# RWKV pairs of a hybrid decoder block: one written list orders the steps of three pairs and the weight stream on all engines

## The chip, the cores and the metric

One Trainium2 chip, one core of it. The metric is the device time of one launch of the kernel in microseconds. Times in tables and traces are microseconds unless marked ns. TensorE multiplies, ScalarE (ACT) and VectorE (DVE) work element by element, GpSimd (POOL) and SyncE (SP) mostly issue transfers here. Each engine takes its instructions in the order in which the program lists them for it, and semaphores make one engine wait for another.

## What is computed

One residual block for a sequence of 512 rows and 2048 channels in fp32. Cut to what matters:

```python
h = rms_norm(x, norm1_g)
z = h @ w_in                                   # 2048 x (RWKV 3*1024+96+96+256, attention 1536, gates 4096)
zs = token_shift(z[..., :RW], rw_mu)           # z + (z_prev - z) * mu
r, k, v, wd, ad, gd = split(zs)
decay = exp(-exp(-softplus(-(w0 + tanh(wd) @ w2)) - 0.5))
a = sigmoid(a0 + ad @ a2);  g = sigmoid(gd) @ g2
kk = normalised(k * k_k);   k = k * (1 + (a - 1) * k_a)
# per head of 64, over the 512 steps:
state = state * w_t + (state @ -kk_t) * (kk_t a_t) + v_t k_t;   y_t = state @ r_t
o_rw = (group_norm(y) + sum(r * k * r_k) * v) * g
o_att = sliding_window_attention(z)
p = sigmoid(zg1) * (o_rw @ w_branch[:1024]) + sigmoid(zg2) * (o_att @ w_branch[1024:])
x = x + p @ w_out
x = x + conv_ffn(rms_norm(x, norm2_g))
```

The change touches the recurrence with its normalisation (o_rw), and the products `h @ w_in` that run beside it.

## The kernel before, in words

The launch goes through stages: the norm and the first products with the attention (up to about 262 us), the RWKV stage (331 to 1168 us), the branch product with w_branch (from 1168 us, "stage B" here), then w_out and the convolutional feed-forward. The change lies in the RWKV stage and in the way into stage B.

**fp32 products.** Every fp32 operand is split into two parts that TensorE multiplies at full rate: hi, a rounded copy that ACT makes, and lo, the remainder that DVE makes by a subtraction. A product is then three matmuls, hi by hi, hi by lo, lo by hi (lines 255, 256, 257). The weights of w_in come as tiles `raw` of 128 x 512 (256 KB) by SP; `load_w` (230) splits one into `whi` (ACT, 238) and `wlo` (DVE, 239), and `project` (244) runs the twelve matmuls (128x512, here "products") that one raw tile feeds. One group of 128 columns of z is four raw tiles, 48 products, into a bank `acc`.

**Pairs.** The sixteen heads are worked in eight pairs of 128 channels, the sequence in NCH = 8 chunks of C = 64 steps. For each pair p there are three functions, and the loop at their end calls late(0), early(1), final(0), three gates, late(1), and so on:

- `early(p)` (from 635): the columns k, r and v of the pair (144 products), the token shift (`shifted`: ACT to `zpad`, DVE to `kz`, `rz`, `vz`), the norm of the key (`head_stats`, a small rsqrt on DVE `rq`, the transposed rows `rsT` that go through DRAM, `rsb`), the low-rank parts of decay and rate, their scans and exponentials (`Ei`, `Et`), and the bonus `bon`.
- `late(p)` (from 690): `BKK` and `BAR`, the two operands of the chunk-wise products; `gram` (719), the 64x64 products within a chunk, masked by DVE to `OW` and `AM` (722); the inverse of a triangular matrix by doubling. Its first level comes from `OW` directly; the transposes of `OW` (729) become `at` (733), split to `AI`, masked to `BT` (741). Then come five levels of two passes. A pass is `mm3` (16 small fp16 matmuls, lines 773 and 774, into the two halves of a PSUM bank) and a DVE `reduce_sum` over the halves (776, 'half'). The first pass (on AI) is masked (790), cast (791) and its remainder taken (792); the second (on BT) scales one half of the result into `BX` on ACT (794) and the other on DVE (795), refreshes `XIW` (797 on ACT, 798 on DVE), and the transposes `id,XIW` (802) are copied back to BT (DVE 806, ACT 808). Beside that DVE scales the keys, `BKK<-BKK,ee` (742, 128x1024), TensorE transposes them (758), ACT copies them to `KD` and `KO` (762, 763); `vz` is transposed and centred (`vm`, `VV`, 746 to 752). Last comes the serial chain over the eight chunks (814 to 828).
- `final(p)` (from 833): outputs of the chunks, their statistics, the scaling `yd` (851), its transposes (855), group norm, the gate's low-rank product `lora6` (618 to 620) and the store `o_rw_d` by POOL (861).

Between them `emit_gate` (357) makes one group of gate columns: 48 products, a tanh on ACT (`gt`, 363), a store. Three gates go with each pair, so a pair holds 6 x 48 = 288 products. The rest comes at the end of the stage: four gates, then the outputs `rin` and the attention's outputs `ain` are loaded by POOL (881, 883) and split (`rhi`, `rlo`, `ahi`, `alo`, 885 to 893) with a gate after every second split.

**Who sets the order.** A list scheduler orders the instructions of each engine by its own estimate of times. Only what is wrapped in `pin` keeps its order in the source among pinned instructions of its engine (the gram, the small matmuls of `heads_mm`, the products of a chain, the splits of stage B). The bank pools: `blk_ps` with 3 banks for everything named `bulk`, `chn_ps` with 2 for the chain, and three more banks for `acc`.

Of the kernel before, what the change touches and what calls it, by code (L numbers as in the profile page):

```python
# [8 lines left out]
F32 = mybir.dt.float32  # L9
F32R = mybir.dt.float32r  # L10
# [18 lines left out]
SQE = float(np.exp(-0.5))  # L29
LEVELS = (1, 2, 4, 8, 16, 32)  # L30
# [99 lines left out]
def block_kernel(ctx: ExitStack, tc: tile.TileContext, d: Dims, a: dict, out: bass.AP):  # L130
# [66 lines left out]
    def free(ins):  # L197
        return ins

# [76 lines left out]
    if True:  # L276
# [243 lines left out]
        with ExitStack() as pr:  # L520
# [4 lines left out]
            blk = pr.enter_context(tc.tile_pool(name="blk_ps", bufs=3, space=PSUM, reuse_waits="tile"))  # L525
            chn = pr.enter_context(tc.tile_pool(name="chn_ps", bufs=2, space=PSUM, reuse_waits="tile"))
# [95 lines left out]
            def heads_mm(dst, l, r, start, stop):  # L622
                for h, (lo, hi) in reversed(list(enumerate(HV))):
                    w = l[lo:hi] if l.shape[-1] == C else l[lo:hi, lo:hi]
                    pin(pe.matmul(dst[lo:hi], w, r[lo:hi], start=start, stop=stop, skip_group_check=True))  # L625

            def bulk_mm(dst, l, r):
                ps = bulk()
                for n in reversed(range(NCH)):
                    heads_mm(r3(ps)[:, n], l(n), r(n), True, True)  # L630
                act.activation(dst, r3(ps), AF.Copy)

            def early(p):
                wl = lp.tile([P, 2 + NG, P], F32, name="wl", tag="wl", bufs=2)
                sync.dma_start(wl, a["lora"][p].rearrange("p (k c) -> p k c", c=P))
                w2a2 = lora_parts(wl, 0)

                acc = ztile(d.c_k + p * P)
                kz = wtile("kz")
                shifted(acc, PR["mu"] + NP + p, kz, 0)  # L640
                kk = wtile("kk")
                dve.tensor_scalar(kk, kz, col("k_k", p), None, op0=ALU.mult)
                sq = wtile("lg")
                act.activation(sq, kk, AF.Square)
                ps = bulk()
                head_stats(ps, sq)
                rs = rsqrt_small(wk, ps[:, 0 : 2 * NT], None, None, mx=1e-24)
                rb = head_rows(wk, bulk(), rs, "lg")
                dve.tensor_tensor(kk, kk, rb, op=ALU.mult)


                ps = bulk()
                lora(ps, w2a2, (0,), 0)
                lg = wtile("lw")
                act.activation(lg, ps, AF.Tanh, scale=0.5)
                dve.tensor_scalar(lg, lg, 1.0, None, op0=ALU.add)
                Ei = wtile("Ei")
                for hs in (slice(0, S // 2), slice(S // 2, S)):
                    dve.tensor_tensor_scan(Ei[:, hs], going, lg[:, hs], 0.0, op0=ALU.mult, op1=ALU.add)
                act.activation(Et[:, :, 1:], r3(Ei), AF.Exp, scale=-0.5 * SQE)  # L660
                act.activation(Ei, Ei, AF.Exp, scale=0.5 * SQE)

                ps = bulk()
                lora(ps, w2a2, (1,), 0)
                ta = wtile("lw")
                act.activation(ta, ps, AF.Tanh, scale=0.5, bias=half[:, 0, p : p + 1])

                acc = ztile(d.c_r + p * P)
                rz = wtile("rz")
                shifted(acc, PR["mu"] + p, rz, 1)  # L670
                acc = ztile(d.c_v + p * P)
                vz = wtile("vz", 2)
                shifted(acc, PR["mu"] + 2 * NP + p, vz, 0)

                k2 = wtile("k2")
                dve.tensor_scalar(k2, ta, half[:, 1, p : p + 1], half[:, 2, p : p + 1], op0=ALU.mult, op1=ALU.add)
                dve.tensor_tensor(k2, k2, kz, op=ALU.mult)
                dve.tensor_scalar(ta, ta, 0.5, 0.5, op0=ALU.mult, op1=ALU.add)
                kb = kz
                dve.tensor_tensor(kb, kk, ta, op=ALU.mult)  # L680
                rk = wtile("lw")
                dve.scalar_tensor_tensor(rk, rz, col("r_k", p), k2, op0=ALU.mult, op1=ALU.mult)
                ps = bulk()
                pe.matmul(ps, K["bo"], rk, start=True, stop=True)
                bon = wtile("bon", 2)
                dve.tensor_tensor(bon, vz, ps, op=ALU.mult)
                act.activation(bon, bon, AF.Identity, bias=col("gn_b", p))
                return wl, Ei, kk, kb, k2, rz, vz, bon

            def late(p, st):  # L690
                wl, Ei, kk, kb, k2, rz, vz, bon = st
                Eex, Ein = Et[:, :, 0:C], Et[:, :, 1:]
                kb3, k23, Ei3, kk3, rz3, vz3 = (r3(x) for x in (kb, k2, Ei, kk, rz, vz))
                dve.tensor_tensor(BKK[:, :, 0:C], kb3, Ei3, op=ALU.mult)
                dve.tensor_tensor(BKK[:, :, C:P], k23, Ei3, op=ALU.mult)
                for h, hs in enumerate(slice(*x) for x in HV):
                    dve.scalar_tensor_tensor(BAR[hs, :, 1 + h], kk3[hs], -1.0, Eex[hs], op0=ALU.mult, op1=ALU.mult)
                dve.tensor_tensor(BAR[:, :, 0], rz3, Ein, op=ALU.mult)
                ee = wk.tile([P, NCH], F32, name="ee", tag="ee")
                act.activation(ee, Et[:, :, C], AF.Copy)  # L700


                XIW = wk.tile([P, 4, NCH, C], F16, name="XIW", tag="rhl")
                X = XIW[:, 0:2]
                CH = C // 2
                IW = XIW[:, 2].rearrange("p n (e c) -> p n e c", e=2)
                tt = wk.tile([P, NCH, C], F32, name="tt", tag="dd")
                HN = NCH // 2

                def mb(nm, n, h=None):  # L710
                    m = K[nm] if h is None else K[nm][h[0] : h[1]]
                    return m.unsqueeze(1).to_broadcast([m.shape[0], n, m.shape[-1]])

                cau = K["cau"].rearrange("p (a c) -> p a c", a=2)
                for n0 in range(0, NCH, HN):
                    gram = [bulk().rearrange("p (n a c) -> p n a c", a=2, c=C) for _ in HV]
                    for j in range(HN):
                        for h, (lo, hi) in enumerate(HV):
                            pin(pe.matmul(gram[h][:, j], BKK[lo:hi, n0 + j], BAR[lo:hi, n0 + j, 0 : 2 + h : 1 + h], start=True, stop=True))
                    for t, rs in ((OW, slice(*HV[0])), (AM, slice(*HV[1]))):  # L720
                        for h, (lo, hi) in enumerate(HV):
                            dve.tensor_tensor(t[lo:hi, :, n0 : n0 + HN].rearrange("p a n c -> p n a c"), gram[h][rs],
                                              cau[rs].unsqueeze(1).to_broadcast([C, HN, 2, C]), op=ALU.mult)
# [739 lines left out]
```

## Time and profile before

| what | value |
|---|---|
| median of 3 runs | 2843.43 us (2840.81 to 2846.24) |
| the profiled execution, own time | 2842.14 us |
| its span | 2839.8 us |
| granted TensorE clock | 0.997 |
| RWKV stage, first `bon` matmul to first product of stage B | 331.5 to 1167.96 us |
| transposes of `yd` (855), once in a pair, start | 420.4, 520.0, 618.8, 717.5, 816.4, 915.3, 1014.3, 1106.9 us |

The profile lists for every engine the instructions with start and length, and for each wait the instruction that ended last before it. PEld is the loading of weights into TensorE, which runs beside its matmuls. A matmul 128x512 is shown with 0.39 us, but the next one may start before that has passed, so the distance of starts is what counts. The period of a pair is the distance of two starts of the same instruction, 98.8 us between the middle pairs.

### The profile page before, as it was taken

What the parts mean: (1) busy time and instruction counts of PE and PEld (TensorE: products, weight loads), DVE (VectorE), ACT (ScalarE), POOL (GpSimd) and SP (SyncE); (2) the same over time, 40 slices, a digit from 0 to 9 for tenths busy, and PEclk for the clock granted to TensorE, in tenths of its full rate; (3) what the DMA queues carried; (4) which work ended last, traced back from release to release, by engine and by line L of the source; (5) the groups of instructions that cost most, each with busy time, mean ns of one, the idle gap of its engine ahead of it and who ended that gap; (6) DMA issues with size and microseconds to landing.
All of it is one profiled execution on the core that took longest, in us unless ns stands there. A gap on an engine that the chain in (4) does not pass through costs nothing.

```text
span 2839.8 us, 48133 instructions
## 1 busy us (share of the span) xinstructions
PE 2772.6 (98%) x18722; PEld 2413.2 (85%) x18722; DVE 1975.7 (70%) x3312; ACT 1289.0 (45%) x2075; POOL 230.8 (8%) x307
## 2 busy tenths in 40 slices
PE   7999999999999999999999999999999999999999
PEld 6888777777777777788888999999999999788887
DVE  5566677778777774455668777777777778655555
ACT  5345344334433433322465555555555555444444
POOL 0101000000000001011000101010101110000000
PEclk9999999999999999999999999999999999999999
DMA  6865676676667668888777789888988897877775
GB/s 190 232 155 152 174 181 166 159 179 162 164 152 177 164 173 240 241 245 275 245 260 200 220 237 245 225 226 232 244 229 224 231 241 227 313 242 241 257 257 189
DMA packets 223860, 608.06 MB, mean 214 GB/s; under 512 B 24576, under 2 KB 44688, under 8 KB 222608
## 3 DMA queue, kind: packets, MB, share of 16 engines
q1 hardware_dynamic: 156096, 432.49, 47.4%
q0 software_dynamic: 36832, 134.24, 24.6%
q10 hardware_dynamic: 30704, 38.27, 3.9%
q8 instruction: 146, 2.39, 0.3%
q14 instruction: 82, 0.67, 0.1%
HBM read 554.23 MB, written 174.40 MB: 257 GB/s over the span
## 4 chain that ended last, share of the span: by engine, by line
PE 86%; DVE 8%; DMA 2%; issue 1%; ACT 1%; ACTq 0%; SPq 0%; DVEq 0%
PE X L1164 18%; PE X L1031 11%; PE acc L255 9%; PE acc L257 9%; PE acc L256 9%; PE Y L1031 9%; PE Y L1164 8%; PE Z L1164 4%; PE bulk L625 1%; PE bulk L773 1%; DMA raw<-in_w_z_dram 1%; PE mi L508 1%; DMA raw<-in_w_dn_dram 1%; DVE BT L741 1%; PE bulk L802 1%
## 5 line engine op out<-in xcount | busy, mean ns | idle before, releaser
L257 PE MATMUL acc<-xhi,wlo 128*128 128x512 f32 x1120 | 450.3, 402 | 6.8 <-DVE wlo L239 6.8
L255 PE MATMUL acc<-xhi,whi 128*128 128x512 f32 x1120 | 450.1, 402 | 2.4 <-ACT whi L238 2.4
L256 PE MATMUL acc<-xlo,whi 128*128 128x512 f32 x1120 | 449.1, 401 | 0.0
L238 ACT ACTIVATE whi<-raw 128x512 fp32r<-128x512 f32 x352 | 220.7, 630 | 466.7 <-PE acc L256 353.3
L1024 DVE TENSOR_TENSOR wlo<-raw,whi 128x1024 fp32r<-128x1024 f32 x210 | 257.1, 1225 | 205.9 <-ACT whi L1023 204.3
L239 DVE TENSOR_TENSOR wlo<-raw,whi 128x512 fp32r<-128x512 f32 x352 | 240.3, 688 | 183.2 <-ACT whi L238 177.3
L1023 ACT ACTIVATE whi<-raw 128x1024 fp32r<-128x1024 f32 x210 | 222.6, 1060 | 291.0 <-PE X L1031 154.2
L1164 PE MATMUL X<-b,whi 128*128 128x256 f32 x1472 | 269.2, 283 | 2.3 <-DVE u L1184 0.9
L1147 DVE TENSOR_TENSOR wlo<-raw,whi 128x1024 fp32r<-128x1024 f32 x176 | 215.1, 1223 | 76.8 <-ACT whi L1146 76.5
L1164 PE MATMUL X<-t,whi 128*128 128x256 f32 x1408 | 259.1, 284 | 8.8 <-DVE u L1184 8.3
L1164 PE MATMUL Y<-t,whi 128*128 128x256 f32 x1408 | 257.1, 283 | 0.0
L257 PEld LDWEIGHTS acc<-xhi,wlo 128*128 128x128 f32 x1120 | 211.6, 189 | 46.4 <-DVE wlo L239 10.7
L255 PEld LDWEIGHTS acc<-xhi,whi 128*128 128x128 f32 x1120 | 211.4, 189 | 40.2 <-ACT whi L238 2.8
L256 PEld LDWEIGHTS acc<-xlo,whi 128*128 128x128 f32 x1120 | 211.8, 189 | 36.0
L1146 ACT ACTIVATE whi<-a 128x1024 fp32r<-128x1024 f32 x132 | 139.4, 1056 | 214.7 <-DVE a L1140 213.3
L1164 PEld LDWEIGHTS X<-b,whi 128*128 128x128 f32 x1472 | 229.5, 192 | 3.1 <-issue 2.4
L1164 PEld LDWEIGHTS X<-t,whi 128*128 128x128 f32 x1408 | 221.0, 193 | 9.3 <-DVE u L1184 5.7
L1164 PEld LDWEIGHTS Y<-t,whi 128*128 128x128 f32 x1408 | 219.6, 192 | 0.0
L1164 PE MATMUL X<-b,wlo 128*128 128x256 f32 x736 | 208.4, 283 | 2.1 <-DVE wlo L1147 2.1
L1147 DVE TENSOR_TENSOR wlo<-a,whi 128x1024 fp32r<-128x1024 f32 x132 | 161.7, 1226 | 67.4 <-ACT whi L1146 66.7
L1164 PE MATMUL X<-t,wlo 128*128 128x256 f32 x704 | 200.1, 284 | 0.0
L1164 PE MATMUL Y<-t,wlo 128*128 128x256 f32 x704 | 199.2, 283 | 0.0
(680 smaller groups left out, 5870.3 us busy)
## 6 DMA issues: line engine op xcount, KB each, us to landing
raw<-in_w_up_dram SPq DMA_DIRECT2D x180, 512.0 KB
raw<-in_w_z_dram SPq DMA_DIRECT2D x288, 256.0 KB
s_dn<-in_w_dn_dram POOLq DMA_DIRECT2D x88, 512.0 KB, 6.5
raw<-in_w_up_dram POOLq DMA_DIRECT2D x88, 512.0 KB, 8.3
raw<-s_dn SPq DMA_DIRECT2D x88, 512.0 KB
raw<-in_w_dn_dram SPq DMA_DIRECT2D x66, 512.0 KB
a<-in_w_up_dram SPq DMA_DIRECT2D x48, 512.0 KB
s_dn<-in_w_dn_dram SPq DMA_DIRECT2D x44, 512.0 KB
```

What stands on the lines that cost most here:

```text
L238: pin(act.activation(hi, raw, AF.Copy))
L239: pin(dve.tensor_tensor(lo, raw, hi.bitcast(F32), op=ALU.subtract))
L255: pe.matmul(acc, whi[:, j], xhi[:, k], start=first, stop=False)
L256: pe.matmul(acc, whi[:, j], xlo[:, k], start=False, stop=False)
L257: pe.matmul(acc, wlo[:, j], xhi[:, k], start=False, stop=last)
L508: pe.matmul(ps[:, h], pT[:, kb, h], vt[:, n - 1 + kb, g * HD : (g + 1) * HD], start=kb == kbs[0], stop=kb == kbs[-1])
L1023: act.activation(whi, wr, AF.Copy)
L1024: dve.tensor_tensor(wlo, wr, whi.bitcast(F32), op=ALU.subtract)
L1031: pe.matmul(dst, l[:, q, ts], r[:, es], start=fst and j == 0, stop=lst and j == 2, skip_group_check=True)
L1146: pin(act.activation(hi, t, AF.Copy))
L1147: pin(dve.tensor_tensor(lo, t, hi.bitcast(F32), op=ALU.subtract))
L1164: pin(pe.matmul(ps, l[:, k], r[:, k], start=start and k + i == 0, stop=last and i == 2, skip_group_check=True))
```

## The change

All work of a pair becomes steps. Three classes stand for the three roles that a pair has one after the other, and one string, the same for every pair, lists which step comes next. A role's method is a generator and does as much as lies up to its next `yield` when its name comes up.

- `Early(p + 1)` ("next"), `Pair(p)` ("now") and the former `Pair` ("gone", for `scaled`, `back` and `gate`, its last three steps) are walked by one list. So the last steps of a pair lie within the list of the pair behind it.
- `Stream` is the weights' stream: `h` makes a whi, `l` a wlo and asks SP for the next raw tile, a number n runs n products, `g` one tanh of a gate. The numbers in one pass of the list add up to 288. All gates that follow go through the stream, so the later `emit_gate` calls find nothing left, and the splits of `rin` are in one piece.
- `Held` pins every instruction of TensorE, ACT and DVE, so the list is the order on them (all of them then have line 224).
- A pass is no longer a reduce on DVE, but a copy of one half on ACT and an addition of the other half on DVE (`summed`). Both halves of BX are scaled on ACT.
- The eight transposes of X come in one piece, and so do those of the keys and the sixteen matmuls of each half of the gram; `AM` goes before `KO` in the chain's inputs.
- `blk_ps` has 4 banks, `chn_ps` 1.
- At the start, pair 0's early part takes 192 products between its steps; after the last pair `scaled`, 30 products, `back`, 12, `gate`, and what is left of the products (102) follow.

The diff, cut to its core:

```diff
+PLAN = """
+gram0 scaled gram0 gram1 h*2 1 gram0 gram1 l 4 gram0 1 gram1 l 7 open 5 turn 3 turn 1 turn 1 h 2 gram0 1 gram1 h open
...
+class Held:
+    def __init__(self, engine):
+        self.engine = engine
+    def __getattr__(self, name):
+        f = getattr(self.engine, name)
+        return f if name.startswith("dma") else lambda *args, **kw: pin(f(*args, **kw))
...
-            blk = pr.enter_context(tc.tile_pool(name="blk_ps", bufs=3, space=PSUM, reuse_waits="tile"))
-            chn = pr.enter_context(tc.tile_pool(name="chn_ps", bufs=2, space=PSUM, reuse_waits="tile"))
+            blk = pr.enter_context(tc.tile_pool(name="blk_ps", bufs=4, space=PSUM, reuse_waits="tile"))
+            chn = pr.enter_context(tc.tile_pool(name="chn_ps", bufs=1, space=PSUM, reuse_waits="tile"))
...
+            class Stream:
+                def hi(self):
+                    if self.raws:
+                        raw = self.raws.pop(0)
+                        hi, lo = (wp["hl"].tile([P, 512], F32R, name=nm, tag=nm) for nm in ("whi", "wlo"))
+                        act.activation(hi, raw, AF.Copy)
+                        self.his.append((hi, lo, raw))
+                def lo(self):
+                    if self.his:
+                        hi, lo, raw = self.his.pop(0)
+                        dve.tensor_tensor(lo, raw, hi.bitcast(F32), op=ALU.subtract)
+                        self.parts.append([w.rearrange("p (k c) -> p k c", c=P) for w in (hi, lo)])
+                        self.load()
...
-                    t = wk.tile([P, NCH, C], F32, name="half_", tag="dd")[:, :, :CH]
-                    dve.reduce_sum(t, p4.rearrange("p n e c -> p n c e"), axis=AX.X)
-                    return t
+                def summed(self, p4):
+                    t = wk.tile([P, NCH, C], F32, name="half_", tag="dd")[:, :, :CH]
+                    act.activation(t, p4[:, :, 1], AF.Copy)
+                    yield
+                    dve.tensor_tensor(t, t, p4[:, :, 0], op=ALU.add)
+                    yield
+                    return t
...
-                    dve.tensor_scalar(altered(BX[C:P, :, C:P]), by_block(t[C:P]), 1.0 / (SG * SG), None, op0=ALU.mult)
+                    act.activation(self.altered(BX[C:P, :, C:P], m), t[C:P], AF.Copy, scale=1.0 / (SG * SG))
...
-            st = early(0)
-            for p in range(NP):
-                lt = late(p, st)
-                if p + 1 < NP:
-                    st = early(p + 1)
-                final(p, lt)
-                for _ in range(GATES_PER_PAIR * NK // 16):
-                    emit_gate()
+            while len(stream.parts) < 2:
+                stream.hi()
+                stream.lo()
+            for p in range(NP):
+                do, st = Pair(st), Early(p + 1) if p + 1 < NP else None
+                Steps(now=do, gone=gone, next=st).run(PLAN)
+                gone = do
+            at_once(gone, "scaled")
+            stream.run(30)
+            at_once(gone, "back")
+            stream.run(12)
+            at_once(gone, "gate")
+            stream.run(10 ** 6)
```

**DVE, around the scaling of the keys.** `BT<-AI,cst` are the masks of 128x1024, `wlo` the weights' remainders, `vm` and `VV` the centred values, `half` the sum of a pass. Before:

```order
L202 TENSOR_TENSOR AI<-at__6907,AI 64x8x64
L738 TENSOR_SCALAR BX<-tt 64x8x64
L741 TENSOR_TENSOR BT<-AI,cst 64x16x64
L202 TENSOR_TENSOR AI<-at__6907,AI 64x8x64
L742 TENSOR_TENSOR BKK<-BKK,ee 128x1024
L741 TENSOR_TENSOR BT<-AI,cst 64x16x64
L748 TENSOR_REDUCE vm<-bulk 128x8
L239 TENSOR_TENSOR wlo<-raw,whi 128x512
L749 TENSOR_SCALAR vm<-vm 128x8
L239 TENSOR_TENSOR wlo<-raw,whi 128x512
```

And in the changed kernel, around the same scaling, which stands in the second pass of level 2 there:

```order
L224 TENSOR_TENSOR wlo<-raw,whi 128x512
L224 TENSOR_TENSOR VV<-bulk,vm 64x4x64
L224 TENSOR_TENSOR wlo<-raw,whi 128x512
L224 TENSOR_TENSOR half__7377<-half__7377,bulk 128x8x32
L224 TENSOR_TENSOR BKK<-BKK,ee 128x1024
L224 SCALAR_TENSOR_TENSOR XIW<-half__7377,XIW 128x64x4
L224 TENSOR_SCALAR rq_7411<-bulk 128x8
```

The scaling has moved from between the two masks, before the first pass, to behind the addition of a second pass, and no mask stands beside it; the remainders before it belong to weights that are used later.

**DVE, the first pass of level 4.** `half` is the pass's sum, `half<-half,cst` its mask, `CAST XIW` and `XIW<-half,XIW` the two parts that TensorE needs for the second pass, `BT<-bulk` the copies of the turned X. Before:

```order
L806 COPY BT<-bulk 64x8x64
L776 TENSOR_REDUCE half__7180<-bulk 128x8x32
L790 TENSOR_TENSOR half__7180<-half__7180,cst 128x8x32
L806 COPY BT<-bulk 64x8x64
L791 CAST XIW<-half__7180 128x8x32
L239 TENSOR_TENSOR wlo<-raw,whi 128x512
L792 TENSOR_TENSOR XIW<-half__7180,XIW 128x8x32
```

In the changed kernel:

```order
L224 TENSOR_TENSOR wlo<-raw,whi 128x512 x2
L224 TENSOR_TENSOR half__7575<-half__7575,bulk 128x8x32
L224 COPY BT<-bulk 64x8x64
L224 TENSOR_TENSOR half__7575<-half__7575,cst 128x8x32
L224 COPY BT<-bulk 64x8x64
L224 CAST XIW<-half__7575 128x8x32
L224 TENSOR_TENSOR XIW<-half__7575,XIW 128x8x32
```

The reduce has become an addition (its other operand is ACT's copy), the remainder of a weight has left the pass, and both BT copies lie within it.

**ACT, the end of the stage.** `gt` is the last gate, `ahi` the first part of the attention's output, `rhi` the parts of the RWKV outputs that stage B multiplies first. Before:

```order
L201 ACTIVATE rhi<-rin_12170 128x512
L201 ACTIVATE rhi<-rin_12171 128x512
L238 ACTIVATE whi<-raw 128x512 x4
L363 ACTIVATE gt<-acc 128x512
L364 DMA gate_d<-gt 128x512
L201 ACTIVATE rhi<-rin_12172 128x512
L201 ACTIVATE rhi<-rin_12173 128x512
L363 ACTIVATE gt<-acc 128x512
L201 ACTIVATE ahi<-ain_12166 128x512
L364 DMA gate_d<-gt 128x512
L201 ACTIVATE rhi<-rin_12174 128x512
L201 ACTIVATE rhi<-rin_12175 128x512
```

In the changed kernel:

```order
L224 ACTIVATE whi<-raw 128x512 x2
L224 ACTIVATE gt<-acc 128x512
L227 ACTIVATE ahi<-ain_12796 128x512
L719 DMA gate_d<-gt 128x512
L227 ACTIVATE rhi<-rin_12798 128x512
L227 ACTIVATE rhi<-rin_12799 128x512
```

The other six rhi follow these two. All eight now stand behind the last gate and the first ahi; before, two did.

More of the change, by code (lines that the diff above doesn't have):

```diff
@@ L624, in heads_mm @@
                     w = l[lo:hi] if l.shape[-1] == C else l[lo:hi, lo:hi]
[L625 to L716, printed above, removed]
@@ L723, in late @@
+                            dve.tensor_tensor(t[lo:hi, :, n0 : n0 + HN].rearrange("p a n c -> p n a c"), g[h][rs],
                                               cau[rs].unsqueeze(1).to_broadcast([C, HN, 2, C]), op=ALU.mult)
[L724 to L729 removed]
@@ L770, in mm3 @@
+                def mm3(self, wt, both, high):
                     ps = bulk()
@@ new lines, in back, with gate @@
+                def back(self):
+                    ps = bulk()
+                    for t in range(NT):
+                        pe.transpose(ps[:, t * P : (t + 1) * P], self.yd[:, t].rearrange("p h c -> p (h c)"), ident)
+                    yield
+                    self.yc = wtile("gn")
+                    dve.scalar_tensor_tensor(self.yc, ps, col("gn_w", self.st.p), self.st.bon, op0=ALU.mult, op1=ALU.add)
+                def gate(self):
+                    parts = lora_tiles()
+                    yield from apart(*parts, self.st.wl[:, 2 : 2 + NG])
+                    ps = bulk()
+                    lora(ps, parts, tuple(range(NG)), 2)
+                    yield
+                    dve.tensor_tensor(self.yc, self.yc, ps, op=ALU.mult)
+                    pool.dma_start(o_rw_d[self.st.p], self.yc)
@@ new lines, in block_kernel, with at_once @@
+            ROLES = {name: role for cls, role in ((Early, "next"), (Pair, "now")) for name in vars(cls)}
+            ROLES.update(scaled="gone", back="gone", gate="gone")
+            def at_once(who, *names):
+                for name in names:
+                    for _ in getattr(who, name)():
+                        pass
+            for _ in range(4):
+                stream.load()
+            st = Early(0)
+            for names, n in (
+                (("fetch", "loras"), 3 * NK),
+                (("krows", "norms"), NK),
+                (("unit", "decay"), 2 * NK),
+                (("rrows",), NK),
+                (("rate", "dense", "rates"), 2 * NK),
+                (("vrows",), 2 * NK),
+                (("bonus",), NK),
+            ):
+                at_once(st, *names)
+                stream.run(n)
```

533 lines of the change are left out of this document (416 added, 117 removed).

## The prediction

> **What bounds the kernel now.** I read the page's busy times first, then the busy times of the stretch that the change rewrites (331 us, the first matmul of pair 0's own work, to 1168 us, the first product of the stage behind) and of one pair in it.
>
> ```profile
> PE 2772.6 (98%) x18722; PEld 2413.2 (85%) x18722; DVE 1975.7 (70%) x3312; ACT 1289.0 (45%) x2075; POOL 230.8 (8%) x307
> ```
> ```profile
> 331.00:1168.00 837.00, 811.56 (x6221) 634.17 (x6220) 600.68 (x1335) 328.09 (x659) 66.83 (x87) 1.00 0.69 175
> 618.80:717.50 98.70, 96.01 (x755) 75.03 (x755) 74.55 (x168) 39.53 (x80) 7.09 (x9) 1.00 0.68 166
> ```
>
> The first five figures behind the window's length are busy us of PE, PEld, DVE, ACT and POOL, and 1.00 is the granted clock. TensorE is the bound: in 837 us it is unoccupied for only 25. So a new order can win no more than TensorE's waits, and the waits of the two queues of TensorE (its matmuls, then its weight loads) in this stretch say where they are.
>
> ```profile
> PE bulk L758 <- DVE BKK L742: 8.2, 8, 1.1
> PE acc L257 <- DVE wlo L239: 6.8, 8, 0.8
> PE bulk L855 <- DVE yd L851: 3.6, 8, 0.5
> PE acc L255 <- ACT whi L238: 2.4, 1, 2.4
> ```
> ```profile
> PEld L773 <- issue: 15.5, 31, 0.8
> PEld L802 <- ACT XIW L797: 11.5, 32, 0.5
> ```
>
> Columns: us in all, times, the longest. Three waits come once in each of the eight pairs. The matmul rows understate them, as the timeline of one place shows (start, duration, count at the end, wait in brackets):
>
> ```profile
> 642.68 0.39 PE L256 MATMUL acc<-xlo,whi 128*128 128x512 f32 x1
> ...
> 644.72 0.39 PE L256 MATMUL acc<-xlo,whi 128*128 128x512 f32 x1
> 646.13 1.06 PE L758 MATMUL bulk<-ident,BKK 128*128 128x128 f32 x8 [1.01 <-DVE BKK L742]
> 646.95 0.48 PE L257 MATMUL acc<-xhi,wlo 128*128 128x512 f32 x1
> 647.26 0.40 PE L255 MATMUL acc<-xhi,whi 128*128 128x512 f32 x1
> ```
>
> Nine products start between the first two rows, 2.04/9 = 0.227 us apart, though each is shown 0.39 long. So the lost time is the distance of starts less 0.227: 1.41 - 0.23 = 1.18 where the row says 1.01. Each shown wait is 0.16 short. The first product behind a group of small matmuls takes 0.31 (646.95 to 647.26), 0.09 more than its like. [...]
>
> Why VectorE is late there is seen in its own timeline:
>
> ```profile
> 644.75 1.23 DVE L742 TENSOR_TENSOR BKK<-BKK,ee 128x1024 f32<-128x1024 f32 x1
> 646.01 1.22 DVE L741 TENSOR_TENSOR BT<-AI,cst 64x1024 f16<-64x1024 f16 x1
> 647.27 0.69 DVE L748 TENSOR_REDUCE vm<-bulk 128x8 f32<-128x512 f32 x1
> 647.99 0.69 DVE L239 TENSOR_TENSOR wlo<-raw,whi 128x512 fp32r<-128x512 f32 x1
> ```
>
> Both costly waits are one congestion: the key scaling, a mask of 1.22 and a reduce stand in a row, and the next weight's remainder (wlo) stands behind them, while VectorE as a whole has a quarter of the pair free (74.55 of 98.70).
>
> **What goes, part by part.** Each wait goes if the new list gives VectorE its operand earlier, and each has been looked up there.
>
> *Keys.* 8.2 + 8 x 0.16 = 9.5. In the new list the scaling comes a level and a half later, right behind the sum of the second level's second pass. Before the transposes TensorE then has four more products and four small matmuls, 4 x 0.23 + 0.4 + 0.09 = 1.4 (0.4, since eight transposes take 0.82, from 646.13 to 646.95), against 1.23 for the scaling: covered, by little.
>
> *Weights.* 6.8 + 8 x 0.16 = 8.1. The remainders now stand one or two weights (12 to 24 products, 2.7 to 5.4 us) ahead of use, and the masks are apart.
>
> *Centred rows.* 3.6 + 1.3 = 4.9: the four yd stand 5 to 25 products ahead of their transposes, which are in the following pair's list now.
>
> *Passes.* The 27.0 us of weight-load idleness (15.5 + 11.5) lie partly under running matmuls. Between nothing and 27.0, I take what the starts of the matmuls show, for which a few rows of levels 1 and 2 stand here (653.69 is the last matmul of a first pass, 662.96 the first of a second):
>
> ```profile
> 653.69 0.18 PE L774 MATMUL bulk<-XIW,AI 128*128 128x32 f16 x1
> ...
> 658.02 0.39 PE L256 MATMUL acc<-xlo,whi 128*128 128x512 f32 x1
> 658.45 0.40 PE L802 MATMUL bulk<-id,XIW 128*128 128x128 f16 x4
> ...
> 662.46 0.39 PE L255 MATMUL acc<-xhi,whi 128*128 128x512 f32 x1
> 662.96 0.19 PE L773 MATMUL bulk<-XIW,BT 128*128 128x64 f16 x1
> ```
> ```profile
> 653.91 0.69 DVE L776 TENSOR_REDUCE half__7006<-bulk 128x256 f32<-128x512 f32 x1
> 654.63 0.42 DVE L790 TENSOR_TENSOR half__7006<-half__7006,cst 128x256 f32<-128x256 f32 x1
> 655.09 0.29 DVE L791 CAST XIW<-half__7006 128x256 f16<-128x256 f32 x1
> 655.42 0.42 DVE L792 TENSOR_TENSOR XIW<-half__7006,XIW 128x256 f16<-128x256 f32 x1
> ```
>
> Beyond 0.227 a second pass waits up to 0.27 (662.96); 40 of them at 0.22, a little less, make 8.9. The transposes between levels wait 0.20 at 658.45; 32 of them at half of that make 3, of which I take 2.8. Together 11.7. All of it goes only if the new gaps between passes cover the path, which is weighed below.
>
> *The rest.* The late weight near the end, 2.4 + 0.1 = 2.5, because fewer products stand there; and 37 instead of 40 runs of products in a pair, 3 x 8 x 0.09 = 2.1. What goes is 9.5 + 8.1 + 4.9 + 11.7 + 2.5 + 2.1 = 38.8.
>
> **What comes.** *The passes' sum.* The reduce of 0.69 becomes an ACT copy of one half and a VectorE add. Neither is in the trace at this shape; the nearest are
>
> ```profile
> L762 ACT ACTIVATE KD<-bulk 64x256 f32<-64x256 f32 x4 | 1.5, 377 | 1.0 <-PE bulk L758 1.0
> ```
>
> for the copy, and 654.63's 0.42 for the add. A dependent VectorE operation starts 0.04 behind the former (654.63 + 0.42 to 655.09), so the step is 0.38 + 0.04 + 0.42 = 0.84 for 0.69: 0.15 longer in 80 passes, at most 12 us if nothing hides it, and 0 if all is hidden; VectorE itself does 0.27 less each time. [...]
>
> Whether it is hidden is counted at the tightest level, the fourth: from the last matmul 0.22 to the reader (653.69 to 653.91), copy 0.42, add, mask and two interposed BT copies at 0.46, cast 0.33, difference 0.42, and 0.06 to TensorE: 3.3. Over it TensorE has twelve products (2.7), the turning of X (0.45, as 658.45 and its second half), a small transpose (0.2) and one restart (0.09): 3.4. That is a tie; the other levels have 12 to 18 products, one of them again close to a tie. I take 0.6 us per pair for ties that miss, 4.8, with 0 and 16 as ends (16: two of the ten passes 1 us short in each pair).
>
> *The end of the stage.* All gates now run inside the stream, and the weights' products end with 102 behind the last pair's gate. The ACT queue there is gate, attention input (ahi), eight rhi. Before, six of the eight rhi were done among the gates. Rows at that place:
>
> ```profile
> 1168.15 0.60 ACT L363 ACTIVATE gt<-acc 128x512 f32<-128x512 f32 x1 [5.05 <-PE acc L257]
> 1168.65 0.62 ACT L201 ACTIVATE ahi<-ain 128x512 fp32r<-128x512 f32 x1
> ...
> 1169.19 1.15 ACT L201 ACTIVATE rhi<-rin 128x512 fp32r<-128x512 f32 x2
> ```
> ```profile
> 1167.96 0.39 PE L255 MATMUL acc<-rhi,whi 128*128 128x512 f32 x1
> ```
> ```profile
> 1109.97 0.59 POOL L861 DMA_DIRECT2D o_rw_d<-gn  x1 [10.47 <-DVE gn L860]
> 1114.48 0.83 POOL L223 DMA_DIRECT2D s_dn<-in_w_dn_dram  x1 [3.92 <-DMA s_dn<-s_dn]
> ...
> 1124.10 0.77 POOL L883 DMA_DIRECT2D ain<-o_at_d  x1 [0.69 <-DMA rin<-o_rw_d]
> ```
> ```profile
> DMA to landing us min/median/max: 12.9/14.4/15.9
> ```
>
> With everything landed, the first rhi would be ready at 1169.8 and its remainder, behind that of ahi on VectorE, at 1170.7: TensorE waits 2.7 where it waited 0. The attention input was issued 14.1 us behind the last output's store, and at least 12.9 more passed to its landing (the last row, of that tile's two transfers), 27 in all, against 102 x 0.227 = 23 of products. The weight-sum transfer that held POOL for 3.9 stands behind six of the loads now, which brings it to about 23: a tie once more. I take 2.7 + 1.3 = 4.0; ends 2.7 and 8.
>
> *The stream's loads.* ACT is held to the list's order, so a late weight stops all behind it. 1.0; ends 0 and 6.
>
> *Without cost:* the moved halves of BX, some 1.9 us of VectorE to ACT per pair, ACT being at 40%; one chain bank instead of two, since the chain uses them one after the other; the fourth bulk bank.
>
> **Sum.** -38.8 + 4.8 + 4.0 + 1.0 = -29.0. The profiled execution took 2842.14 (2839.8 of it the span), so 2813.1; it lies 1.3 under 2843.43, the median of the runs, so 2814.
>
> **Rivals.**
>
> *VectorE becomes the bound in a pair's first third (slower).* Until the first second pass the list gives VectorE 20 operations of 0.69, 12 of 0.42, two masks of 1.22, the twelve small ones of the rsqrt (below) and a cast: 13.8 + 5.0 + 2.4 + 2.0 + 0.3 = 23.5 us, over 26.9 of TensorE's (94 products at 0.227, and some 5.6 of small matmuls).
>
> ```profile
> L190 DVE TENSOR_TENSOR rq<-rq 128x8 f32<-128x8 f32 x6 | 1.0, 166 | 0.1
> ```
>
> The margin of 3.4 has to hold every wait of VectorE there, and in a fixed order it can do nothing else meanwhile: at least 1.0 for the transposes of OW and something for the gram. If the waits come to 9 us, each pair is 5.6 longer, 45 in all: 2814 + 45 = 2859. It turns to slower from 3.6 per pair (29.0/8). For it: VectorE took the blame for most waits. Against: the known waits are under 2. Chance 0.09.
>
> *The passes miss their cover.* Three or four of ten passes short by 0.7 to 1 in each pair, 3 us x 8 = 24 in place of 4.8: 2833. For it: ties above, and a copy on ACT that may stand behind a weight's whi (0.6, the form of ahi). Chance 0.15.
>
> *The end waits for its loads.* 8 in place of 4.0, and 6 in place of 1.0 for late weights: 2823. For it: 27 against 23. [...] Chance 0.12.
>
> *The list does little.* If the order were in effect the old one, the same congestion would be met: 2843. The listed order on VectorE and ACT differs in nearly every row, so 0.04 is enough.
>
> **How the numbers follow.** Forecast 0.60, the rivals 0.09, 0.15, 0.12, 0.04. The forecast's own ends are 2842.14 - 38.8 + 2.7 + 1.3 = 2807 and, with the passes' own 11.7 half gone only, 2820; an order that removes more than the counted waits (the smaller ones are left out above) could give a few us below. The range 2800 to 2838 holds the forecast and two rivals and leaves out the slower and the unchanged. What a measurement of this kernel tells from no change is some 0.2%, 5.7 us. Faster: 0.60 + 0.15 + 0.12 less a little for what I can't see, 0.84; the same 0.06; slower 0.10.
>
> **What would show it.** Right: the three waits of eight gone from TensorE's list, the pair's period near 95 from 98.7, and the only new wait of size at the first rhi, 3 to 5 us. Wrong: a wait of TensorE on VectorE of several us in each pair around the first passes; a period over 97.5; or a wait at the first rhi of 8 and more.

## The result, and the profile after

The changed kernel takes 2820.71 us (median of 4 runs, 2818.63 to 2822.04), the kernel before 2842.5 on the same chip. The ratio is 0.9921, with a 95% interval from 0.9904 to 0.9938. The forecast was 2814 in a range from 2800 to 2838. The profiled execution took 2819.42, its span is 2817.6.

Where the 22.2 us of span come from, by the starts of the first gram matmul of each pair and of the first product of stage B, in both traces (48 products, 10.9 us, have moved from behind the first gram to ahead of it and are put to the stretch where they were):

| stretch | before | after | difference |
|---|---|---|---|
| up to the first gram | 332.4 + 10.9 | 342.2 | -1.1 |
| the first to the eighth gram, seven pairs | 693.6 | 663.8 | -29.8 |
| the eighth gram to stage B | 141.9 - 10.9 | 135.5 | +4.5 |
| stage B to the end | 1671.8 | 1676.1 | +4.3 |

The last steps of a pair (the transposes of `yd` and the gate's products) now lie in the list of the pair behind it. So the first pair's stretch lacks them, 93.25 us against 95.1 for the others, and the last stretch has them twice: 1.9 us of the -29.8 and of the +4.5 have only changed places. The pairs gave 28, and the end of the stage took nearly 7 of it back. The period of a middle pair went from 98.8 to 95.1.

The waits of TensorE's matmuls in the changed kernel, 320 to 1160 us (us in all, times, longest):

```profile
PE bulk L224 <- DVE XIW L224: 18.4, 25, 1.2
PE acc L281 <- ACT rhi L227: 6.4, 1, 6.4
PE bulk L224 <- DVE BKK L224: 0.5, 1, 0.5
```

The three waits that came once in each pair (BKK, wlo, yd) are gone, but for one at BKK. Two others take their place: the second passes wait for XIW, and stage B waits once for the rhi. The row for XIW was 0.7 before, but it understates. The distances of starts ahead of the forty second passes, less 0.227 each, sum up to 9.4 us before. For the changed kernel they are measured against the run with the last copy later, below, in which these matmuls start without a wait: 23.1 us more. In a middle pair that is 1.29 at level 2, 0.25 at level 3, 0.69 at level 4 and 0.64 at level 5, together 2.87.

The place in a pair that waits longest, by the three engines, on each a few rows of the fourth pair. TensorE, the second pass of level 2:

```profile
661.68 0.39 PE L224 MATMUL acc<-xhi,wlo 128*128 128x512 f32 x1
663.20 0.26 PE L224 MATMUL bulk<-XIW,BT 128*128 128x64 f16 x4 [1.13 <-DVE XIW L224]
```

VectorE in the same stretch:

```profile
658.16 0.42 DVE L224 TENSOR_TENSOR half__7322<-half__7322,bulk 128x256 f32<-128x256 f32 x1 [1.16 <-ACT half__7322 L224]
658.50 0.41 DVE L224 COPY BT<-bulk 64x512 f16<-64x512 f16 x1
660.57 0.43 DVE L224 COPY BT<-bulk 64x512 f16<-64x512 f16 x1 [1.66 <-ACT BT L224]
661.03 0.43 DVE L224 TENSOR_TENSOR half__7322<-half__7322,cst 128x256 f32<-128x256 f32 x1
661.49 0.42 DVE L224 TENSOR_TENSOR VV<-bulk,vm 64x256 f32<-64x256 f32 x1
661.93 0.29 DVE L224 CAST XIW<-half__7322 128x256 f16<-128x256 f32 x1
```

And ACT:

```profile
657.75 0.38 ACT L224 ACTIVATE half__7322<-bulk 128x256 f32<-128x256 f32 x1 [2.84 <-PE bulk L224]
658.15 0.63 ACT L224 ACTIVATE whi<-raw 128x512 fp32r<-128x512 f32 x1
658.69 0.62 ACT L224 ACTIVATE lg<-kk 128x512 f32<-128x512 f32 x1
659.33 1.21 ACT L224 ACTIVATE BT<-bulk 64x512 f16<-64x512 f16 x2
```

The sum of the pass is ready at 658.58. Its mask could start then, but VectorE stands at its second BT copy, which waits for ACT's two BT copies, and these stand behind a weight and a square. The mask starts at 661.03. In the list the second BT copy is ahead of the mask, so VectorE idles 1.66 us with work at hand.

The end of the stage, on ACT and on POOL:

```profile
1135.20 0.60 ACT L224 ACTIVATE gt<-acc 128x512 f32<-128x512 f32 x1 [7.45 <-PE acc L224]
1140.32 0.63 ACT L227 ACTIVATE ahi<-ain 128x512 fp32r<-128x512 f32 x1 [4.52 <-DMA ain<-o_at_d]
...
1140.86 4.25 ACT L227 ACTIVATE rhi<-rin 128x512 fp32r<-128x512 f32 x8
```
```profile
1116.15 3.51 POOL L1210 DMA_DIRECT2D rin<-o_rw_d  x6
1125.70 0.88 POOL L249 DMA_DIRECT2D s_dn<-in_w_dn_dram  x1 [6.04 <-DMA s_dn<-s_dn]
1126.27 1.44 POOL L1210 DMA_DIRECT2D rin<-o_rw_d  x2
1127.34 1.88 POOL L1212 DMA_DIRECT2D ain<-o_at_d  x2
```

The attention's input lands at 1140.3, 13 us behind its issue, and POOL had issued it late because it stood 6 us at a weight-sum transfer between the loads. ACT waits for it with eight rhi behind it. TensorE, whose last product started at 1134.78, stands until 1141.53. What follows is seen by windows of that stretch (busy us of PE, PEld, DVE, ACT, POOL, then the granted clock):

```profile
1134.80:1141.50 6.70, 0.37 (x2) 0.00 (x0) 0.52 (x1) 1.77 (x4) 0.92 (x1) 0.88 1.03 403
1141.50:1146.40 4.90, 4.88 (x12) 3.70 (x13) 4.90 (x9) 4.90 (x10) 0.00 (x0) 0.50 1.05 319
1146.80:1157.00 10.20, 10.20 (x46) 8.43 (x45) 7.69 (x13) 4.38 (x8) 0.00 (x0) 1.00 0.73 245
```

Behind the wait the clock is 0.50 for five microseconds, and products start 0.43 us apart instead of 0.23.

### The profile page after: what moved, and what is told of

It reads as the page before. It is cut to its first block, busy times and chain, and to the rows that moved or that the text cites. A ratio compares the mean times of both kernels' runs of the same rounds, so it can differ in the third digit from the quotient of the medians.

```text
span 2817.6 us, 47988 instructions
## 1 busy us (share of the span) xinstructions
PE 2748.3 (98%) x18722; PEld 2426.8 (86%) x18722; DVE 1926.5 (68%) x3264; ACT 1335.3 (47%) x2203; POOL 229.4 (8%) x307
## 4 chain that ended last, share of the span: by engine, by line
PE 87%; DVE 4%; ACT 3%; DMA 2%; issue 1%; ACTq 0%; POOL 0%; SPq 0%; DVEq 0%; POOLq 0%
PE X L1493 17%; PE acc L224 17%; PE X L1360 11%; PE Y L1360 9%; PE Y L1493 8%; PE bulk L224 5%; PE acc L281 4%; PE acc L282 4%; PE acc L283 4%; PE Z L1493 4%; PE acc L698 2%; PE link L224 1%; ACT BT L224 1%; PE mi L534 1%; DMA raw<-in_w_dn_dram 1%
## 5 line engine op out<-in xcount | busy, mean ns | idle before, releaser
L1352 ACT ACTIVATE whi<-raw 128x1024 fp32r<-128x1024 f32 x210 | 222.6, 1060 | 290.5 <-PE X L1360 155.4
L224 PE MATMUL acc<-xlo,whi 128*128 128x512 f32 x816 | 328.7, 403 | 0.0
L224 PE MATMUL acc<-xhi,whi 128*128 128x512 f32 x816 | 327.8, 402 | 0.0
L224 PE MATMUL acc<-xhi,wlo 128*128 128x512 f32 x816 | 327.6, 401 | 0.0
L1475 ACT ACTIVATE whi<-raw 128x1024 fp32r<-128x1024 f32 x176 | 184.3, 1048 | 18.6 <-ACT whi L1475 14.7
L1360 PE MATMUL X<-whi,hhi 128*128 128x512 f32 x480 | 187.7, 391 | 0.9 <-ACT u L1509 0.7
L1360 PE MATMUL X<-whi,hlo 128*128 128x512 f32 x480 | 188.1, 392 | 0.0
L1360 PE MATMUL X<-wlo,hhi 128*128 128x512 f32 x480 | 187.4, 390 | 0.5 <-DVE wlo L1353 0.5
L224 PEld LDWEIGHTS acc<-xhi,whi 128*128 128x128 f32 x816 | 153.7, 188 | 27.8
```

Source lines behind the costliest of these rows:

```text
L224: return f if name.startswith("dma") else lambda *args, **kw: pin(f(*args, **kw))
L1352: act.activation(whi, wr, AF.Copy)
L1360: pe.matmul(dst, l[:, q, ts], r[:, es], start=fst and j == 0, stop=lst and j == 2, skip_group_check=True)
L1475: pin(act.activation(hi, t, AF.Copy))
```

## The experiments

All ratios are to the kernel before on the same chip; each edit is one of the changed kernel, unless it says otherwise.

**A weight and a square behind the copies.** In the list, at level 2:

```diff
-values turned1 first2 h krows first2 1 turned1 4 turned1*3 h 2 first2
+values turned1 first2*2 1 turned1 4 turned1*3 h krows h 2 first2
```

> The changed kernel with one edit in its list: at level 2 the weight's whi and the square of the key stand behind the two ACT copies of BT instead of ahead of them. Theory A (VectorE stands idle before its second BT copy because ACT works off 0.63 + 0.62 us first, and the pass's mask stands behind that copy): the idle time of 1.66 us there falls to about 0.5, TensorE's wait of 1.28 us before that second pass goes, 8 x 1.28 = 10 us less, some 2811 where the changed kernel has 2820.7. Rival B (the pass is late because its own six steps are longer than its cover): the wait stays over 1 us and the time at 2820. Rival C (the square or the weight is now late where it is used): a new wait of over 0.5 us in each pair at the norm or at a product, 2816 or more.

2817.2 us, ratio 0.9907 (0.9893 to 0.9920). The period is 94.7 instead of 95.1; TensorE's wait there 0.90 instead of 1.29. Theory A named the right instruction and too small a part of the cause. VectorE and ACT in this run:

```profile
660.53 0.41 DVE L224 COPY BT<-bulk 64x512 f16<-64x512 f16 x1
662.21 0.43 DVE L224 COPY BT<-bulk 64x512 f16<-64x512 f16 x1 [1.27 <-ACT BT L224]
```
```profile
660.98 1.21 ACT L224 ACTIVATE BT<-bulk 64x512 f16<-64x512 f16 x2 [0.81 <-DVE BT L224]
```

With nothing else ahead in ACT's queue the copies still form a chain: ACT's first waits for VectorE's first, VectorE's second for ACT's second. That chain alone holds VectorE for 1.27 us. The four copies write different elements of BT and read one PSUM tile; which of the two makes them take turns, no run shows. The time by itself doesn't tell this run from the changed kernel, whose second series (at the end) has a ratio of 0.9904; the period and the wait do.

**The last copy behind the difference.** At levels 2 to 5 the mask, cast and difference come ahead of VectorE's last BT copy, and ACT's copies ahead of the weights between them. What else stood between them, at level 2 two operations for the centred rows (`VV`, 0.42 us each), moves behind as well. Of the four places, level 4:

```diff
-first4 1 turned3*2 1 turned3 first4 1 turned3 1 decay 1 first4 1 unit first4 second4
+first4 1 turned3*2 1 turned3 first4 1 first4*2 turned3 1 decay 1 1 unit second4
```

> The changed kernel with its list edited at levels 2 to 5: mask, cast and difference of the first pass stand ahead of VectorE's last BT copy, and ACT's two BT copies ahead of the weights that stood before or between them. Nothing else is changed. Theory A (these four waits of TensorE come from VectorE's wait for ACT's BT copies alone): all four go, 2.36 us in a pair, 19 us in all, some 2802. Rival B (the path of the pass is too long for its cover in itself): only the wait of level 2 gets shorter, by 0.5 to 1.3 us, 2810 to 2817. Rival C (a weight or key copy moved behind is late): waits of over 0.5 us appear elsewhere in each pair, and the gain is under 8 us.

2796.85 us, ratio 0.9837 (0.9824 to 0.9851): 24 under the changed kernel, 21 under its second series, more than the 19 of theory A. That sum was counted short: at levels 4 and 5 it took 0.38 and 0.45, where the same matmuls start 0.69 and 0.64 us earlier here. With these the four waits are 2.87 in a pair, and the period is 92.25, 2.85 less than 95.1. VectorE's wait for ACT's BT copies over the whole stage (331 to 1141 us), in the kernel before, in the changed one, and in this one:

```profile
DVE BT L806 <- ACT BT L808: 2.0, 9, 0.5
```
```profile
DVE BT L224 <- ACT BT L224: 42.9, 32, 1.7
```
```profile
DVE BT L224 <- ACT BT L224: 3.7, 24, 0.2
```

And TensorE's waits in this one:

```profile
PE acc L281 <- ACT rhi L227: 5.7, 1, 5.7
PE bulk L224 <- DVE XIW L224: 1.5, 1, 1.5
PE acc L224 <- DVE wlo L224: 1.1, 1, 1.1
```

18.4 us of waits for XIW have become 1.5, once, in the last pair, whose list has no next pair to fill it. The passes had their cover all along (as many products stand in each gap as before); what they lacked was VectorE, which stood in its queue. At levels 3 to 5 only the second BT copy stood between mask and cast; at level 2 this run doesn't tell the copy from the two VV operations. Rivals B and C fall.

**The reduce back, in the changed kernel.** `summed` becomes one VectorE reduce again:

```diff
-                    act.activation(t, p4[:, :, 1], AF.Copy)
                     yield
-                    dve.tensor_tensor(t, t, p4[:, :, 0], op=ALU.add)
+                    dve.reduce_sum(t, p4.rearrange("p n e c -> p n c e"), axis=AX.X)
```

> The changed kernel with one part undone: each pass sums by one VectorE reduce over the two halves again (0.69 us), with no copy on ACT, at the same place in the list. Theory A (the passes wait for ACT's queue, VectorE has time): each BT copy of ACT comes 0.4 us earlier, the waits before the second passes (1.28, 0.25, 0.38, 0.45 in a pair) shrink by about that: 1.1 us in a pair, 9 us in all, some 2812. Rival B (VectorE's own work sets the passes): 0.27 us more on VectorE in each of ten passes lengthens the pair by up to 2 us, some 2830 or more. If both cancel, 2820.

2815.62 us, ratio 0.9903 (0.9889 to 0.9916); its period is 94.7, the waits in a pair 0.77, 0.78, 0.61 and 0.24 instead of 1.29, 0.25, 0.69 and 0.64. That is 0.46 less in a pair, under half of what theory A expected, and one of the four has grown. In time the run can't be told from the changed kernel's second series (0.9904). So the splitting of the sum was no gain in this order, and no large loss.

**The attention's splits behind the rhi.**

```diff
-                split(ahi[:, i], alo[:, i], ain[2 * i // NQ][:, i % (NQ // 2)])
+                split(ahi[:, i], alo[:, i], ain[2 * i // NQ][:, i % (NQ // 2)], pin)
```

> The changed kernel with one edit: the attention's splits are held behind the eight rhi on ACT and VectorE. Theory A (the first ahi waits for its transfer and holds up the rhi, whose operands are there): TensorE's 6.5 us before stage B fall to about 2 (gate 0.6, rhi 0.6, remainder 0.7), its granted clock there stays at 1.00 instead of 0.52, so that the first eleven products start 0.23 and not 0.43 us apart: 4.5 + 2.3 = 6.8 us less, some 2814. Rival B (the outputs' own loads land late as well, all of them being held up on POOL): a wait of over 4 us stays, on the loads of rin, and the gain is under 2.5 us.

2813.19 us, ratio 0.9894 (0.9880 to 0.9907). The wait before stage B and the clock behind it:

```profile
PE acc L281 <- ACT rhi L227: 1.8, 1, 1.8
```
```profile
1131.94:1135.35 3.41, 2.86 (x13) 2.05 (x11) 0.00 (x0) 0.51 (x1) 0.00 (x0) 1.00 1.01 335
1135.35:1138.76 3.41, 2.15 (x8) 1.49 (x9) 2.17 (x4) 2.92 (x7) 0.92 (x1) 1.00 1.02 394
1138.76:1142.18 3.42, 3.42 (x17) 2.82 (x16) 3.42 (x7) 3.42 (x7) 0.00 (x0) 1.00 1.04 404
```

Theory A, in both parts: 1.8 us of waiting and a clock of 1.00. The rhi's operands had been there, but for 0.49 us of ACT's waiting for the first; ACT's order had kept them.

**Both, and both with the reduce.** The edits of the two runs above together; and the same with the reduce.

> The changed kernel with both edits that paid: VectorE's last BT copy behind the difference at levels 2 to 5, and the attention's splits behind the rhi. Theory A (the two losses are apart, one in each pair, one at the end): they add up, 2820.7 - 23.9 - 7.5 = some 2789. Rival B (a stage that ends 20 us earlier meets its loads later, so the wait before stage B grows back): over 4 us stay there and the time is 2793 or more.

2791.91 us, ratio 0.9820 (0.9806 to 0.9833): the losses add up, nearly. The wait for the rhi stays 1.8, but the clock behind it is 0.50 for 3.41 us here, where the run with the same wait above has 1.00, and the first twelve products of stage B take 4.70 us instead of 3.14:

```profile
1113.38:1116.79 3.41, 1.60 (x7) 0.71 (x5) 0.84 (x2) 2.09 (x4) 0.00 (x0) 1.00 1.03 421
1116.79:1120.20 3.41, 3.41 (x8) 2.67 (x9) 3.41 (x7) 3.41 (x8) 0.92 (x1) 0.50 1.03 396
```

> The kernel of the run beside it (copies and rhi moved), with each pass summed by one VectorE reduce again. Theory A (once VectorE no longer waits for ACT's BT copies, the passes have cover either way and the split of the sum decides nothing): within 3 us of the run beside it. Rival B (the copy and the addition are longer by 0.15 us in a pass and that shows): 5 to 12 us faster than it. Rival C (VectorE is the bound of a pair and needs its 0.27 us in each pass): slower than it by 5 us or more.

2788.89 us, ratio 0.9813 (0.9799 to 0.9826); the intervals of the two overlap, and the periods are 92.21 to 92.25 and 92.21. Theory A: with VectorE free the passes are covered with either sum, and the split of it decides nothing.

**The split of the sum alone, in the kernel before.**

```diff
-                    dve.reduce_sum(t, p4.rearrange("p n e c -> p n c e"), axis=AX.X)
+                    act.activation(t, p4[:, :, 1], AF.Copy)
+                    dve.tensor_tensor(t, t, p4[:, :, 0], op=ALU.add)
```

> The kernel before with one part of the change alone: each pass sums by an ACT copy of one half and a VectorE addition; the scheduler orders everything as it sees fit. Theory A (the part is worth little by itself, and the gain comes from the list): within 8 us of 2842. Rival B (VectorE's congestion was the bound, 2.7 us less of it in a pair is the gain): 2830 or less. Rival C (0.15 us more on the path of each of 80 passes, which TensorE waits for in the old order): 2850 or more.

2844.69 us, ratio 1.0005 (0.9996 to 1.0014): theory A. Its waits of TensorE:

```profile
PE bulk L773 <- DVE XIW L793: 10.4, 34, 0.6
PE bulk L758 <- DVE BKK L742: 8.3, 8, 1.1
PE acc L257 <- DVE wlo L239: 6.7, 8, 0.8
PE bulk L856 <- DVE yd L852: 3.6, 8, 0.5
```

The three waits of eight stand as they were (8.2, 6.8 and 3.6 before): the 0.27 us that VectorE saves in each pass doesn't remove them. Rival C's mechanism is seen, though not its time: by distances of starts the second passes wait 17.1 us here and 9.4 before. Since the scheduler reorders the rest too, the run doesn't price the longer path of a pass by itself.

**The idle time before stage B filled.** The rhi are as late as in the changed kernel; TensorE multiplies the identity meanwhile, result unused:

```diff
+            idle = accp.tile([P, S], F32, name="idle", tag="acc")
+            for _ in range(60):
+                pin(pe.matmul(idle[:, :P], ident, ident, start=True, stop=True))
```

> The changed kernel with sixty small fp32 matmuls (128x128 on the identity, about 0.11 us each, 6.5 us in all, their result unused) on TensorE between the last product and stage B. Theory A (the half speed of the first products of stage B is the granted clock's answer to 6.5 us without matmuls): the rhi are no earlier, but the clock stays at 1.00 and the products behind start 0.23 us apart from the first; 2.3 us less, 2818. Rival B (these products wait for their operands, one remainder of 0.6 us for three products): they start 0.43 us apart again, 2820.

> The changed kernel with 28 small fp32 matmuls before stage B instead of sixty. The sixty turned out as 120 rows and 13.5 us, longer than the wait; 28 should take 6.3 us and fill it just so. Theory A (the granted clock answers to the idle time): the first product of stage B starts within 1 us of where it did, at the end of the fill, and those behind it 0.23 us apart, clock 1.00. Rival B (they wait for their remainders): 0.4 us apart for three or more of the first twelve, clock 1.00 or not.

Sixty took 13.6 us, twice what was meant, so that stage B, at 1149.60, started some 7 us later than the rhi would have let it. Its products start 0.23 us apart from the second on, at a clock of 1.00, and the first twelve take 2.85 us, where the changed kernel takes 5.26 and the kernel before 2.72. But the operands are all there by then, so this alone does not tell idle time from late operands. Twenty-eight took 6.4 us and ended at 1142.6, but the rhi came at 1144.1 in that run, so 1.6 us of idle time stayed:

```profile
1136.18 6.41 PE L1202 MATMUL idle<-ident 128*128 128x128 f32 x56
1144.15 0.49 PE L281 MATMUL acc<-rhi,whi 128*128 128x512 f32 x1 [1.55 <-ACT rhi L227]
1144.96 0.50 PE L282 MATMUL acc<-rlo,whi 128*128 128x512 f32 x1 [0.31 <-DVE rlo L228]
1145.30 0.40 PE L283 MATMUL acc<-rhi,wlo 128*128 128x512 f32 x1
...
1146.00 0.50 PE L283 MATMUL acc<-rhi,wlo 128*128 128x512 f32 x1
1146.30 0.63 PE L281 MATMUL acc<-rhi,whi 128*128 128x512 f32 x1
```

Behind the two waits the products start 0.23 apart, with the operands just made; then, from 1146.30 to 1149.29, 0.43 apart with no wait shown, at a clock of 0.50. So the slow starts are the clock's and not the operands', against rival B. Theory A's clock of 1.00 isn't met either: the waits that remained sufficed (the last section shows how). The times, 2822.98 and 2823.55, are of single runs and decide nothing here.

**The last gate behind the rhi.** The tanh of the last gate, the last instruction ahead of the first rhi on ACT, is moved behind the eight rhi in the kernel with both edits and the reduce.

> The kernel with both edits and the reduce, and the tanh of the last gate behind the eight rhi on ACT, so that these are made while the last products run. Theory A (what is left of the wait before stage B, 2.0 us, is the chain gate, first rhi, first remainder behind the last product): it falls below 0.5 us if the first outputs have landed by then; 2 us less than that kernel. Rival B (the last of the outputs' loads lands too late and ACT stands at its rhi, with the gate and the attention's splits behind it): a wait of 1 us or more among the first 24 products of stage B or behind them, no gain.

2792.8 us, ratio 0.9811 (0.9796 to 0.9825): no gain. Stage B starts without a wait, and 48 products later there is one of 2.9:

```profile
1121.66 0.39 PE L283 MATMUL acc<-rhi,wlo 128*128 128x512 f32 x1
1124.96 0.50 PE L281 MATMUL acc<-ahi,whi 128*128 128x512 f32 x1 [2.91 <-ACT whi L264]
```

The clock drops behind this wait too (0.50 from 1125.96 to 1129.37): the twelve products from 1124.96 on take 5.0 us instead of 2.7. Now the next weight's whi is late. It stands behind the attention's splits on ACT, and these wait for their transfer (3.32 us ahead of the first four, 3.45 ahead of the other four). That is rival B in part: not the outputs' loads, but the attention's.

**The changed kernel again**, unaltered.

> The changed kernel unaltered, on the chip of this call: 2820 within 3 us, to compare the edits with; 0.8% under the kernel before.

2818.32 us, ratio 0.9904 (0.9888 to 0.9921), with the same period of 95.1 and the same wait for XIW (18.4).

## Why the prediction was right, and where its steps were not

The direction, the range and the period of a pair near 95 were met: 2820.71 lies in 2800 to 2838. That the number came so close is in good part luck: two terms were wrong by about 18 us each, in opposite directions. Of the prediction's own signs of being right, "the only new wait of size at the first rhi, 3 to 5 us" was not met: that wait is 6.5, and a larger new one, 2.87 us in each pair, stands at the second passes. The steps that carry it:

- *Keys, weights and centred rows.* Right. 9.5 + 8.1 + 4.9 were to go, and the rows are gone but for 0.5 in the last pair. The split of the sum alone leaves all three standing, so it is the rest of the change that removes them. That it is the list is read from VectorE's order; the bank counts (`blk_ps`, `chn_ps`) and the halves of BX moved to ACT were not tried apart.
- *The passes.* Mis-sized: "I take 0.6 us per pair for ties that miss", with 16 as the upper end of the stage. Measured, by distances of starts, are 1.29 + 0.25 + 0.69 + 0.64 = 2.87 in a pair, 23.1 in the stage, beyond that end. The step that failed is the count of the fourth level's path, "two interposed BT copies at 0.46": it took the second of them as 0.46 us of work, where it is a wait for another engine (0.94 us idle there at level 4, 1.60 and 1.25 at levels 3 and 5, 1.66 at level 2). The rival "the passes miss their cover" came true in place and size (four of ten passes, 23 where it has 24); its time of 2833 was missed because of what was not counted. It had not the cause, since the run with the last copy later shows that there is cover enough. The copy that that rival saw behind a weight was ACT's copy of the sum; the ones that mattered were ACT's copies into BT.
- *What was not counted.* With 23.1 instead of 4.8 the period should have been 97.3, and it is 95.1. The starts of one pair's matmuls, summed by kind, give 0.9 us less in the chain's small matmuls, 0.4 in the gram, 0.2 in the low-rank products. Before, TensorE's weight loads waited in the chain; these rows the prediction left out:

```profile
PEld psS L827 <- ACT UU L821: 10.3, 41, 0.3
PEld psG L814 <- DVE SS L828: 9.7, 35, 1.0
PEld psU L820 <- DVE G L816: 7.2, 34, 0.2
```

  Of those 27 us the changed kernel shows 4.4 in all, under the name link. That three to four products between two links, instead of two to three, are the cause was only argued; no run tells it apart.
- *The end of the stage.* Mis-sized: 4.0, "ends 2.7 and 8". Measured are 6.5 of waiting and 4.3 more behind it, 10.8. The wait was foreseen as a mechanism (ahi ahead of the rhi, an input that lands at a tie), and moving the splits took 5 to 7.5 us off (against the two series of the changed kernel). It was put too low because the transfer that holds POOL was thought to cost nothing once behind six of the loads: it stands ahead of the attention's input, for 6.04 us. The clock was read (1.00 in both windows) and then forgotten: behind 6.5 idle us of TensorE its clock was 0.50 for five more, and the first twelve products of stage B take 5.26 us instead of 2.72. The rest of the 4.3, 1.7 us, belongs to no step of the prediction: it falls some 410 us later, at a wait for VectorE's `u` in the feed-forward, where the gap between two starts is 6.98 us (5.79 before) and the clock stays at 0.50 for 10.2 us behind it (6.8 before). That gap is 5.8 to 7.5 us in these runs, and 7.18 in the kernel before with only the sum split.
- *The stream's loads.* 1.0 was allowed; TensorE's waits in the changed kernel hold none for a whi, so nothing.
- *The slower rival*, VectorE as the bound of a pair's first third: no wait of TensorE appears before the first pass of level 1. It falls.

The terms sum up: -38.8 gone, -17 uncounted, +23.1 passes, +10.8 end, -22 in all, the 22.2 us of span. The 17 is what is left over; the pair's matmuls show 1.5 x 8 = 12 of it, 1.1 lies ahead of the first gram, and some 4 is not placed. The forecast of -29.0 was off by some 6.5, about what the end was off by (10.8 for 4.0). The errors of the passes (18.3 too little) and of what was not counted (17) cancelled, which no step of the prediction foresaw.

The best of these kernels, the list with the last copies and the splits moved, runs in 2789 to 2792 us, 0.981 to 0.982 of the kernel before, so the change as made got about two fifths of what the best of these lists gets.

## What to carry to other kernels

In an order that is fixed, an instruction that waits costs its engine all that stands behind it (here VectorE's second BT copy waited 1.66 us with the mask behind it, ACT's first ahi 4.52 us with eight rhi behind it): put the operation whose operand comes from another engine's queue behind the ones on the critical path, even if it looks like half a microsecond of work. Count a step in such a queue by what it waits for, and look at each engine on which its operand is made for what stands ahead there. When the last piece of a stage becomes short, look at what used to be hidden under it: loads, splits, and the clock of an engine that now stands idle (here TensorE's was 0.50 behind the 6.5 us).

## What was not expected of the hardware

TensorE's granted clock fell to half behind gaps far shorter than the 6.5 us of the changed kernel: for 3.41 us behind 2.2 us between starts in the run with both edits, and behind waits of 1.55 and 0.31 us in the run with 28 fillers, while a gap of 2.2 us left it at 1.00 in the runs with the splits moved and with both edits and the reduce. The traces show what tells these apart. In each of the thirteen traces every drop of the clock stands on one grid of 3.41 us that runs through the whole execution. Take the idle time of TensorE in one step of that grid as the distances of starts beyond 0.227 us, where a distance is over 0.5. From 331 us on, each step at full clock with 1.92 us of it or more is followed by half clock, 34 in all, and none with 1.83 or less is. In the run with both edits the gap lies within one step, 1113.38 to 1116.79, with 1.97 us of idle time; with the splits moved it lies across the edge at 1135.35, 0.7 us on one side and 1.26 on the other. So in this kernel the same gap costs some 1.5 us or nothing, by where it falls on the grid. This was read from finished traces: no edit moved a gap across an edge, and ahead of 331 us, among the attention's smaller matmuls, the clock also dropped where this count is lower.

And the small fp32 matmuls on the identity took two rows each, 0.11 us a row, where one was assumed. So 128 columns of whole fp32 took 0.23 us, as long as the 512 columns of a product of the split parts (0.227); small fp16 matmuls of 128 columns start 0.055 us apart in the kernel before, nearly the same time a column as in the products.
